# Feed-forward of a hybrid decoder layer: engines in program order, weight splits three products ahead

## The chip, the cores and the metric

The kernel runs on one core of a Trainium2 chip. The metric is the device time of one execution in microseconds (us), the median of several runs. A profiled execution gives the trace from which all other times here are read.

## The reference

One layer of a causal decoder over 2048 tokens of width 1024, in float32:

```
h = x + W_out [ GLA_heads(n) ; DilatedSWA_heads(n) ],  n = RMSNorm(x)
h = h + W_ff2 ( relu( RMSNorm(h) W_ff1 ) ** 2 )        # W_ff1: 1024 x 4096, W_ff2: 4096 x 1024
y = RMSNorm_final(h)
```

Both mixers (gated linear attention and dilated sliding-window attention) lie ahead of everything that is changed. The change concerns the second line and the final norm.

## The kernel before

**Splits.** Every float32 operand of a matrix product is kept as two parts: a high half, rounded by a copy on ScalarE (line 415), and a low half, the difference, made by a subtraction on VectorE (line 416). `mm3` (lines 135 to 137) then makes three matmuls of each block: high by high, low by high, high by low. So a product can start when its high half is there, and goes on when the low half is.

**First feed-forward matrix.** It is multiplied by a scheme with seven products in place of eight, on blocks of two by two. A group is one weight block of 256 columns (`g`, 32 groups: 16 weight blocks for each half of the tokens); its seven products (`j` in the order 1, 2, 5, 6, 3, 4, 7) are numbered through by `at`, 0 to 223. One product is 12 matmuls into one PSUM bank; eight banks go round.

`prep1(at)` makes the split of the weights of product `at` into one of four slots, so it waits until product `at - 4` has been read. Weight differences for later products of the group are made in place in the raw block by VectorE: line 1159 with the second product, lines 1161 and 1162 with the third, 1164 with the fourth. With the seventh product the load of the block two groups on is issued (line 1144, SyncE's queue); there are two raw blocks.

`product1(at)` issues the matmuls and takes the result out of PSUM: by a copy on ScalarE for the first, third and sixth product of a group (line 1191), by additions on VectorE for the others (lines 1193, 1196 and 1197, 1199, and 1202 to 1204 for the seventh). Finished quarters are run through relu and square on ScalarE (lines 1187 and 1188): one quarter with the second and fifth product, two with the seventh.

**Token sums.** The second matrix uses a scheme with 26 products on blocks of the tokens, so the activations are summed over token blocks: 28 sums for each pair of groups, on GpSimd (line 1229), in the tiles `acc1` and in the free halves of `xt` and `gM` (shown as gs), with stores to memory by SyncE (line 1219). They run three steps a product, spread over the pair of groups that follows.

**Reload.** With the last group of the first token half the other operand is replaced by that of the second half: seven loads (line 1110) and 14 split parts (lines 415 and 416, tile hb), between products 106 and 116.

**Second matrix.** 52 phases of eight steps, two blocks of three matmuls a step. Token splits (`prep_s`, lines 1299 to 1303, tile cs, three slots), weight combinations on GpSimd (`add_t`, line 1322), weight splits (`prep_t`, tile ct, six slots), loads, and the additions of results (`taken`, line 1369) are hung on numbered steps by `at_step`; `step(n)` issues what is due, ahead of that step's matmuls. The first of these steps fall into the last 14 products of the first matrix.

**What sets the order.** Each engine works its queue in order. For most of the program a planner decides that order: it simulates the program and picks the next instruction of each engine by its own estimate. Inside `tc.manual_schedule(engines=...)` the named engines keep the order in which the program issues their instructions. In the kernel before, from the first product on, this holds for SyncE alone:

```
    with tc.manual_schedule(engines={SP.engine}):
        ...
        for at in range(7, len(jobs1)):
            ...
            prep1(at + 2)
            product1(at)
            for _ in range(3):
                next(ts, None)
```

`T`, `V`, `A`, `G` and `SP` are TensorE, VectorE, ScalarE, GpSimd and SyncE.

Of the kernel before, what the change touches and what calls it, by code (L numbers as in the profile page):

```python
# [109 lines left out]
def emit(tc, a, stop=99):  # L110
    nc = tc.nc
    V, A, G, T, SP = nc.vector, nc.scalar, nc.gpsimd, nc.tensor, nc.sync
# [9 lines left out]
    def slot(name, dt=F32, n=SLOT):  # L122

        return up.tile([128, SLOT], dt, name=name, tag="u", bufs=26)[:, :n]

    def view(t, shape):
        n = int(np.prod(shape))
        names = "abcd"[:len(shape)]
        return t[:, :n].rearrange(f"p ({' '.join(names)}) -> p {' '.join(names)}", **dict(zip(names, shape)))
# [284 lines left out]
    def split(hi, lo, src):  # L414
        A.activation(hi, src, AF.Copy)  # L415
        V.tensor_tensor(lo, src, hi.bitcast(F32), op=OP.subtract)  # L416
# [4 lines left out]
    X = {}  # L421
# [89 lines left out]
    def reload(j):  # L511
        t = (xp, bp)[order.index(j) % 2][:, :2048]
        SP.dma_start(t, nTD[j - 1].rearrange("p c s -> p (c s)"))

        def rest():
            for cs in (slice(0, 1024), slice(1024, 2048)):
                split(*[v[:, cs] for v in TF[j]], t[:, cs])

        return rest
# [565 lines left out]
    def norm_to_T(src, dst, t):  # L1085

        normed(src, dst, gM)
        half, i = t // HT, t % 4
        b = [view(bb[:, 512 * q:], (4, 128)) for q in range(4)]
        k = t % HT // 4  # L1090
        for q, pv in enumerate(transposed(dst)):
            A.activation(b[2 * k + q], pv, AF.Copy)
        if k == 0:
            return
        (b11, b21, b12, b22), (t2, t4, t3) = b, [view(tb[:, 512 * q:], (4, 128)) for q in range(3)]
        V.tensor_tensor(b12, b12, b11, op=OP.subtract)
        V.tensor_tensor(t2, b22, b12, op=OP.subtract)
        V.tensor_tensor(t4, b21, t2, op=OP.subtract)
        V.tensor_tensor(t3, t2, b11, op=OP.subtract)
        for j, v in ((1, b11), (2, b21), (5, b12), (6, t2), (3, b22), (4, t4), (7, t3)):  # L1100
            SP.dma_start(hTD[half, j - 1][:, :, i * 128:i * 128 + 128], v)
# [37 lines left out]
    def load_w1(g):  # L1139
        if g < 2 * NP:  # L1140
            if len(raw1) < 2:
                raw1.append(view(slot("w1raw"), (CH, 256)))
            g0 = g % NP * 256
            SP.dma_start(raw1[g % 2], w1[:, :, g0:g0 + 256])

    def prep1(at):

        if at >= len(jobs1):
            return
        g, j = jobs1[at]  # L1150
        if not combs1:
            combs1.extend(view(c[:, 1024 * q:], (2, 4, 128)) for c in [slot("w1comb", FR) for _ in range(2)]
                          for q in range(2))
        r = raw1[g % 2]
        (a11, a12), (a21, a22) = [[r[:, 4 * k:4 * k + 4, n * 128:n * 128 + 128] for k in range(2)] for n in range(2)]
        c = combs1[at % 4]
        split(c[:, 0], c[:, 1], {1: a11, 2: a12, 5: a21, 6: a21, 3: a12, 4: a22, 7: a21}[j])
        if j == 2:
            V.tensor_tensor(a21, a21, a22, op=OP.add)  # L1159
        if j == 5:  # L1160
            V.tensor_tensor(a21, a21, a11, op=OP.subtract)  # L1161
            V.tensor_tensor(a12, a12, a21, op=OP.subtract)
        if j == 6:
            V.tensor_tensor(a21, a22, a21, op=OP.subtract)
        if j == 7:
            load_w1(g + 2)
# [3 lines left out]
    def bank():  # L1170
        tags.append(tags.pop(0))
        return ps(tags[-1])

    def product1(at):
        g, j = jobs1[at]
        half, gh = divmod(g, NP)
        if not acc1:
            acc1.extend(slot("acc1") for _ in range(4))
        X = gM[:, :512] if g % 2 else xt[:, :512]
        c11, c12, c21, c22 = [acc1[g % 4][:, 512 * n:512 * n + 512] for n in range(4)]  # L1180
        p = bank()
        B, W = TB[j], combs1[at % 4]
        for c in range(4):
            mm3(p, W[:, 0, c], W[:, 1, c], B[0][:, c], B[1][:, c], c == 0, c == 3)

        def square(v):
            A.activation(v, v, AF.Relu)  # L1187
            A.activation(v, v, AF.Square)

        if j in (1, 5, 4):  # L1190
            A.activation({1: X, 5: c22, 4: c21}[j], p, AF.Copy)
        elif j == 2:
            V.tensor_tensor(c11, p, X, op=OP.add)
            square(c11)
        elif j == 6:
            V.tensor_tensor(X, p, X, op=OP.add)
            V.tensor_tensor(c12, X, c22, op=OP.add)
        elif j == 3:
            V.tensor_tensor(c12, p, c12, op=OP.add)  # L1199
            square(c12)  # L1200
        else:
            V.tensor_tensor(X, p, X, op=OP.add)
            V.tensor_tensor(c21, c21, X, op=OP.add)
            V.tensor_tensor(c22, c22, X, op=OP.add)
            square(c21)
            square(c22)
# [7 lines left out]
    def token_sums(g):  # L1214

        half, c, t = g // NP, g % NP // 2, act_tiles(g)

        def store(r, v):
            SP.dma_start(actD[r, half, :, c], v)

        for i in range(len(SUMS) + BEHIND):
            if i == 2:
                for l, r in SINGLES:
                    store(r, t[l])
            if i >= BEHIND and SUMS[i - BEHIND][4] is not None:
                store(SUMS[i - BEHIND][4], t[SUMS[i - BEHIND][0]])
            if i < len(SUMS):
                l, x, op, y, _ = SUMS[i]
                G.tensor_tensor(t[l], t[x], t[y], op=OP.add if op == "+" else OP.subtract)  # L1229
            yield  # L1230
# [161 lines left out]
    def step(n):  # L1392
        now[0] = n
        for f, args in steps.pop(n, ()):
            f(*args)
# [21 lines left out]
    with tc.manual_schedule(engines={SP.engine}):  # L1417
        rb.append(slot("rb"))
        back = [*back, reload(order[3], 0), reload(order[4], 0), reload(order[5], 0, slot("rt"))]
        load_w1(1)  # L1420
        for at in range(7):
            if at == 2:
                norm_to_T(*late)
            if back:
                list(back.pop(0))
            if at == 1:
                back.append(reload(order[6], 0))
            prep1(at + 2)
            product1(at)


        first, parts_at = 7 * (NP - 1), {}
        for n in range(14):
            parts_at.setdefault(first + 1 + n * 4 // 5, []).append(n // 2)
        halves, begun = {}, set()
        ts = iter(())
        for at in range(7, len(jobs1)):
            if at == first - 2:
                halves.update({n: reload(order[n], 1) for n in range(2)})
            prep1(at + 2)  # L1440
            product1(at)
            for _ in range(3):
                next(ts, None)
            if at % 14 == 13:
                ts = token_sums(at // 7)
            for n in parts_at.get(at, ()):
                next(halves[n])
                if n in begun and n + 2 < 7:
                    halves[n + 2] = reload(order[n + 2], 1)
                begun.add(n)  # L1450
            for n in range(2):
                step(2 * (at - len(jobs1)) + n)

        P, left = {}, None
        for ph in range(2 * NR):
            if PRODUCTS[ph // 2][1]:
                P[ph % 2] = [bank() for _ in range(2)]
            p = P[ph % 2]
            for k in range(8):
                step(8 * ph + k)  # L1460
                if ph < 4:
                    for _ in range(2 - k % 2):
                        next(ts, None)
                if left and k < 2:
                    taken(ph - 1, k, left[k])
                if ph < 2 * NR - 1 or k < 2:
                    for i in range(2):
                        mm2(p[i], ph, k, i)
            left = p
        for i in range(2):  # L1470
            for k in range(2, 8):
                mm2(left[i], 2 * NR - 1, k, i)
            taken(2 * NR - 1, i, left[i])
# [55 lines left out]
```

## Time and profile before

| what | value |
|---|---|
| median of 3 runs | 2422.37 us (2422.12 to 2425.93) |
| profiled execution | 2425.41 us |
| its span, first to last instruction | 2423.6 us |
| first feed-forward matrix, TensorE | 1124.6 to 1827.9 us |
| second feed-forward matrix, TensorE | 1820.3 to 2416.6 us |
| busy share of the span | TensorE 94%, VectorE 70%, GpSimd 49%, ScalarE 48% |
| mean granted TensorE clock | 0.983 |

How the lines are read. A row of busy time by stretches gives the stretch in us and its length, then for each engine (TensorE, its weight loads, VectorE, ScalarE, GpSimd) the busy us and the number of instructions, then the granted clock, the share of the DMA engines and GB/s. A row of waits gives who waited for whom, the us in total, the number of times, and the longest. A row in order of time gives the start and the length in us, engine, line, operation, what it writes and reads, the shapes, how many instructions are merged, and in brackets the idle time of the engine before it and what ended it. A row of a group gives the count, the busy us and the mean in ns, the idle time before them and what ended it; a row by source line gives shortest, median and longest in ns, and the first and last start. PE is TensorE, PEld its weight load, DVE VectorE, ACT ScalarE, POOL GpSimd, SPq SyncE's queue. L416 is line 416.

### The profile page before, as it was taken

To read this page: it belongs to the slowest core of one execution; us is meant where nothing else is said; L and a number is where in the kernel's file an instruction comes from. 1 tells how busy PE (TensorE), PEld (TensorE's weight loads), DVE (VectorE), ACT (ScalarE), POOL (GpSimd) and SP (SyncE) were. 2 spreads that over 40 slices of the span, in tenths; PEclk is the share of its full clock that TensorE was granted. 3 is DMA by queue.
4 is the path that set the end of the run, shared out by engine and by line. 5 is a ranking of instruction groups with operands and counts; after the bars stand their busy time and mean duration, and the time that the engine had idled before them with its cause. 6 is when DMAs were issued, how large, how long until landed. Compare 5 with 4: busy or idle time off the path is not lost.

```text
span 2423.6 us, 35461 instructions
## 1 busy us (share of the span) xinstructions
PE 2288.7 (94%) x12456; PEld 1956.2 (81%) x12456; DVE 1702.2 (70%) x2802; ACT 1165.8 (48%) x2227; POOL 1182.6 (49%) x1098
## 2 busy tenths in 40 slices
PE   6999999999999998999999988899989999999998
PEld 6977998789999996888877776777767778888777
DVE  6888768766676784447666668565667858858786
ACT  5565436435677771235544446444444334333444
POOL 4333324345478784000476576575664635432564
PEclk9999999999999998999999999999999999999999
DMA  6458744767666873677343455444449554444463
GB/s 155 121 162 251 245 147 122 247 186 238 188 215 227 255 238 117 208 258 227 109 131 121 130 158 195 126 125 139 126 132 328 212 189 159 139 156 130 160 225 111
DMA packets 340368, 430.76 MB, mean 178 GB/s; under 512 B 20772, under 2 KB 270133, under 8 KB 333662
## 3 DMA queue, kind: packets, MB, share of 16 engines
q1 hardware_dynamic: 340046, 428.24, 55.4%
q8 instruction: 98, 1.61, 0.3%
q14 instruction: 80, 0.66, 0.1%
q10 hardware_dynamic: 144, 0.26, 0.0%
HBM read 276.60 MB, written 156.54 MB: 179 GB/s over the span
## 4 chain that ended last, share of the span: by engine, by line
PE 48%; POOL 17%; issue 14%; DVE 10%; DMA 8%; ACT 2%; SPq 2%; POOLq 0%; DVEq 0%; ACTq 0%
POOL acc L1229 8%; PE ps_a L136 5%; PE ps_a L137 5%; PE ps_a L135 5%; PE ps_a L753 4%; POOL gs L1229 3%; PE ps_c L136 3%; PE ps_c L137 3%; PE ps_c L135 3%; PE ps_d L734 3%; DMA rt<-w_ff 2%; PE ps_c L712 2%; PE ps_c L714 2%; DVE ct L416 2%; POOL xt L1229 2%
## 5 line engine op out<-in xcount | busy, mean ns | idle before, releaser
L416 DVE TENSOR_TENSOR w1comb<-w1raw,w1comb 128x512 fp32r<-128x512 f32 x224 | 188.9, 846 | 66.2 <-ACT w1comb L415 66.0
L415 ACT ACTIVATE w1comb<-w1raw 128x512 fp32r<-128x512 f32 x224 | 134.9, 623 | 189.3 <-DVE w1raw L1161 167.1
L725 ACT ACTIVATE pe<-pe,O 128x256 f32<-128x256 f32 (+1 forms) x384 | 156.0, 454 | 56.8 <-DVE O L724 52.2
L753 PE MATMUL ps_a<-v,pt 128*128 128x65 f32 x1200 | 178.7, 250 | 0.7 <-DVE pt L743 0.7
L1299 ACT ACTIVATE cs<-rs 128x1024 fp32r<-128x1024 f32 x104 | 108.5, 1049 | 144.9 <-PE ps_c L137 79.4
L753 PEld LDWEIGHTS ps_a<-v,pt 128*128 128x128 f32 x1200 | 174.6, 193 | 2.2 <-DVE pt L743 0.9
L1229 POOL TENSOR_TENSOR acc<-acc 128x256 f32<-128x256 f32 x160 | 168.5, 1066 | 15.5 <-DMA actD<-acc 15.4
L163 POOL TENSOR_TENSOR stats<-stats,mhalf 128x1 f32<-128x1 f32 (+1 forms) x64 | 45.8, 717 | 255.6 <-DVE stats L162 255.5
L416 DVE TENSOR_TENSOR ct<-rt,ct 128x1024 fp32r<-128x1024 f32 x68 | 120.7, 1783 | 59.9 <-ACT ct L415 59.6
L734 PE MATMUL ps_d<-ident,pe 128*128 128x128 f32 x600 | 159.1, 278 | 0.0
L724 DVE CUSTOM_DVE_ANT_0 pe<-ps_c,nb 128x256 f32<-128x256 f32 (+1 forms) x384 | 126.8, 360 | 42.6 <-PE ps_d L734 18.1
L1187 ACT ACTIVATE acc<-acc 128x512 f32<-128x512 f32 x128 | 80.3, 631 | 142.2 <-DVE acc L1199 72.0
L136 PE MATMUL ps_c<-hb,w1comb 128*128 128x512 f32 x336 | 134.3, 400 | 11.7 <-DVE w1comb L416 11.7
L271 ACT ACTIVATE wcomb<-wraw 128x512 fp32r<-128x512 f32 (+2 forms) x126 | 96.5, 772 | 93.9 <-POOL wraw L277 20.5
L136 PE MATMUL ps_c<-ct,cs 128*128 128x512 f32 x360 | 141.2, 392 | 0.4 <-DVE cs L1303 0.4
L137 PE MATMUL ps_c<-ct,cs 128*128 128x512 f32 x360 | 141.3, 392 | 0.0
L135 PE MATMUL ps_c<-ct,cs 128*128 128x512 f32 x360 | 141.0, 392 | 0.0
L135 PE MATMUL ps_c<-hb,w1comb 128*128 128x512 f32 x336 | 133.5, 397 | 7.5 <-ACT w1comb L415 7.5
L415 ACT ACTIVATE ct<-rt 128x1024 fp32r<-128x1024 f32 x68 | 71.5, 1059 | 132.8 <-POOL rt L1322 79.5
L137 PE MATMUL ps_c<-hb,w1comb 128*128 128x512 f32 x336 | 133.2, 396 | 0.0
L273 DVE TENSOR_TENSOR wcomb<-wraw,wcomb 128x512 fp32r<-128x512 f32 (+2 forms) x84 | 100.5, 1200 | 38.0 <-ACT wcomb L271 37.6
L1159 DVE TENSOR_TENSOR w1raw<-w1raw 128x512 f32<-128x512 f32 x32 | 26.2, 819 | 138.3 <-DMA w1raw<-w_ff 137.2
(375 smaller groups left out, 7916.4 us busy)
## 6 DMA issues: line engine op xcount, KB each, us to landing
rs<-actD SPq DMA_DIRECT2D x103, 512.0 KB, 4.3
actD<-acc SPq DMA_DIRECT2D x288, 128.0 KB, 2.1
w1raw<-w_ff SPq DMA_DIRECT2D x32, 1024.0 KB, 6.6
rt<-w_ff SPq DMA_DIRECT2D x24, 1024.0 KB, 8.3
k<-kD SPq DMA_DIRECT2D x16, 1024.0 KB, 8.3
rb<-hTD SPq DMA_DIRECT2D x13, 1024.0 KB, 6.9
wraw<-w_in SPq DMA_DIRECT2D x48, 256.0 KB, 3.7
cmb<-boD SPq DMA_DIRECT2D x16, 528.0 KB, 6.1
```

The lines of the kernel that those rows point to most:

```text
L135: T.matmul(out, sh, mh, start=first, stop=False, skip_group_check=more)
L136: T.matmul(out, sl, mh, start=False, stop=False, skip_group_check=more)
L137: T.matmul(out, sh, ml, start=False, stop=last, skip_group_check=more)
L273: V.tensor_tensor(lo, src, hi.bitcast(F32), op=OP.subtract)
L415: A.activation(hi, src, AF.Copy)
L416: V.tensor_tensor(lo, src, hi.bitcast(F32), op=OP.subtract)
L724: V.tensor_tensor_reduce(p, s, bias, scale=1.0, scalar=BIG, op0=OP.add, op1=OP.min, accum_out=nm)
L725: A.activation(p, p, AF.Exp, bias=nm, scale=-1.0)
L734: T.transpose(pb[:, i * 128:i * 128 + 128], src, ident)
L753: T.matmul(self.b.opsum[:, n % 4], self.pt[:, i * 128:i * 128 + 128], self.b.v[:, blk, cols], start=first, stop=last)
L1229: G.tensor_tensor(t[l], t[x], t[y], op=OP.add if op == "+" else OP.subtract)
L1299: A.activation(v[:, 0, cs], x, AF.Copy, scale=float(sign))
```

## The change

The loop over products splits into two blocks. The first seven products stay as they were ordered (SyncE alone in program order), but from the fourth on `prep1` runs three products ahead there; at the third the splits of both the fifth and the sixth are made, so that none is left out. From the eighth product on, through the second matrix to the end, all five engines keep program order, and `prep1` runs three products ahead.

```
@@ -1425,10 +1425,12 @@
                 list(back.pop(0))
             if at == 1:
                 back.append(reload(order[6], 0))
-            prep1(at + 2)
+            prep1(at + 2 + (at > 2))
+            if at == 2:
+                prep1(5)
             product1(at)
 
-
+    with tc.manual_schedule(engines={X.engine for X in (T, V, A, G, SP)}):
         first, parts_at = 7 * (NP - 1), {}
         for n in range(14):
             parts_at.setdefault(first + 1 + n * 4 // 5, []).append(n // 2)
@@ -1437,7 +1439,7 @@
         for at in range(7, len(jobs1)):
             if at == first - 2:
                 halves.update({n: reload(order[n], 1) for n in range(2)})
-            prep1(at + 2)
+            prep1(at + 3)
             product1(at)
             for _ in range(3):
                 next(ts, None)
```

The four weight slots are not changed, so a split three ahead goes into the slot of the product just before the one being issued.

More of the change, by code (lines that the diff above doesn't have):

```diff
@@ L1427, in emit @@
                 back.append(reload(order[6], 0))
-            prep1(at + 2)
+            prep1(at + 2 + (at > 2))
+            if at == 2:
+                prep1(5)
             product1(at)
+    with tc.manual_schedule(engines={X.engine for X in (T, V, A, G, SP)}):
         first, parts_at = 7 * (NP - 1), {}
@@ L1439, in emit @@
                 halves.update({n: reload(order[n], 1) for n in range(2)})
-            prep1(at + 2)
+            prep1(at + 3)
             product1(at)
```

## The prediction

> **What bounds the kernel now.** I read the page first, then the busy time by stretches, TensorE's waits in the two feed-forward products, then VectorE's, ScalarE's and SyncE's rows in order of time.
>
> ```profile
> span 2423.6 us, 35461 instructions
> 2000.00:2100.00 100.00, 100.00 (x443) 82.81 (x442) 83.32 (x61) 37.63 (x38) 54.14 (x19) 1.00 0.47 155
> 1828.00:2416.00 588.00, 573.31 (x2494) 471.35 (x2493) 448.35 (x394) 230.91 (x278) 275.06 (x130) 0.99 0.53 179
> 1165.00:1203.00 38.00, 38.00 (x169) 31.47 (x168) 26.77 (x33) 20.95 (x36) 27.37 (x28) 1.00 0.38 120
> 1417.00:1514.00 97.00, 85.08 (x338) 65.12 (x337) 76.62 (x86) 51.78 (x85) 63.60 (x56) 0.95 0.58 189
> PE ps_a L136 <- DVE w1comb L416: 24.6, 13, 3.5
> PE ps_c L136 <- DVE w1comb L416: 11.7, 8, 3.9
> PE ps_d L136 <- DVE w1comb L416: 10.3, 8, 2.8
> PE ps_d L136 <- DVE cs L1301: 5.8, 3, 2.4
> PE ps_d L136 <- DVE cs L1303: 4.4, 2, 3.2
> PE ps_a L136 <- DVE cs L1303: 2.2, 1, 2.2
> PE ps_d L135 <- ACT cs L1299: 1.9, 1, 1.9
> ```
>
> A fully fed TensorE issues 443 matmuls in 100 us, 0.2257 us each. So a product of the first feed-forward matrix (12 matmuls) is 2.71 us, a group of seven 18.96, a pair of groups (the period of the token sums) 37.9; the stretch from 1165 shows one such pair. The second matrix has 2494 matmuls in 588 us where 563 would do: it loses 25 us, 14.3 of them in the four waits listed last. The first three waits are the first matrix's: TensorE stands before the low halves that line 416 makes on VectorE.
>
> ```profile
> 1294.42 0.69 DVE L1159 TENSOR_TENSOR w1raw<-w1raw 128x512 f32<-128x512 f32 x1 [8.61 <-DMA w1raw<-w_ff]
> 1330.97 0.40 SPq L1144 DMA_DIRECT2D w1raw<-w_ff  x1
> 1337.79 0.69 DVE L1159 TENSOR_TENSOR w1raw<-w1raw 128x512 f32<-128x512 f32 x1 [8.04 <-DMA w1raw<-w_ff]
> 1338.40 0.68 DVE L416 TENSOR_TENSOR w1comb<-w1raw,w1comb 128x512 fp32r<-128x512 f32 x1
> 1339.90 0.63 ACT L415 ACTIVATE w1comb<-w1raw 128x512 fp32r<-128x512 f32 x1 [8.42 <-DVE w1raw L1161]
> ```
>
> Why they are late: the planner puts line 1159 of the next weight block ahead of the current block's splits. That block's load is issued only at 1330.97, behind stores of token sums in SyncE's queue; VectorE stands 8.04 us in order, and ScalarE 8.42 behind it. Two such rows, one pair apart, lie 43.4 us apart: the steady pair loses 5.5 us against 37.9.
>
> **The change part by part.** Program order sets line 1159 six products later than the planner does, behind the splits of its own block, so this 8 us wait goes. What is late next? In program order each product puts on VectorE: its eviction, the low half four products on, the weight differences. On ScalarE: copy or two squarings, then the high half four products on. The low half waits for the high half, which stands behind the squarings, which wait for the eviction: VectorE and ScalarE take turns. The price of a turn:
>
> ```profile
> 1322.19 0.68 DVE L1193 TENSOR_TENSOR acc<-ps_a,gs 128x512 f32<-128x512 f32 x1
> 1322.90 0.63 ACT L1187 ACTIVATE acc<-acc 128x512 f32<-128x512 f32 x1 [0.84 <-DVE acc L1193]
> 1323.57 0.63 ACT L1188 ACTIVATE acc<-acc 128x512 f32<-128x512 f32 x1
> 1324.10 0.58 ACT L1191 ACTIVATE acc<-ps_c 128x512 f32<-128x512 f32 x1
> 1324.58 1.66 ACT L415 ACTIVATE w1comb<-w1raw 128x512 fp32r<-128x512 f32 x3
> 1325.23 0.77 DVE L416 TENSOR_TENSOR w1comb<-w1raw,w1comb 128x512 fp32r<-128x512 f32 x1 [1.77 <-ACT w1comb L415]
> ```
>
> From the eviction's start to the squaring's end-of-issue 1.91 (1324.10), then the high half 0.63 and 0.03: 2.57 us until the low half starts. Independent VectorE operations of 0.68 start 0.61 apart (1337.79 and 1338.40; I use 0.60), ScalarE's 0.52 (three in 1.66).
>
> ```profile
> 1311.91 1.13 DVE L1159 TENSOR_TENSOR w1raw<-w1raw 128x512 f32<-128x512 f32 x1 [2.10 <-DMA w1raw<-w_ff]
> 1318.75 1.22 DVE L416 TENSOR_TENSOR w1comb<-w1raw,w1comb 128x512 fp32r<-128x512 f32 x1
> 1320.00 1.11 DVE L1164 TENSOR_TENSOR w1raw<-w1raw 128x512 f32<-128x512 f32 x1
> 1327.13 1.22 DVE L1197 TENSOR_TENSOR acc<-gs,acc 128x512 f32<-128x512 f32 x1
> L1203 DVE TENSOR_TENSOR acc<-acc,xt x16: 689/1222/1226, 1147.6 to 1803.9; 128x512 f32<-128x512 f32 x16
> L1203 DVE TENSOR_TENSOR acc<-acc,gs x16: 682/684/693, 1166.2 to 1830.2; 128x512 f32<-128x512 f32 x16
> L1229 POOL TENSOR_TENSOR acc<-acc 128x256 f32<-128x256 f32 x160 | 168.5, 1066 | 15.5 <-DMA actD<-acc 15.4
> ```
>
> The same line 1203 takes 0.68 when it falls where GpSimd has no sums (tile gs, the pair's end) and 1.22 when it falls among them (tile xt). So a group costs twice. Without sums, from the seventh product's eviction: lines 1202 to 1204 and both pairs of squarings, low half at 4.48; difference 5.20; next low half 5.80; L1193 6.40, a turn, low half 8.97; next 9.97 (its high half stands behind a copy); L1196 and L1197 from 10.57; low half 11.88; L1199 12.48, a turn, 15.05; L1159 15.65, whose result the next high half reads: low half 17.01; L1161 17.73, L1162 18.45; next eviction at 19.05. That is TensorE's own 18.96. Among the sums, of the 14 operations of a group that read SBUF twice, 9 are long (over 1 us) in the group whose first and last long ones are the rows at 1311.91 and 1327.13; two of them I take to lie behind ScalarE's part, so 7 x 0.52 = 3.6 is added: 22.7. Bounds: 4 long ones (only those directly behind another) 21.1, 11 of them 24.8. The 28 sums of a pair last 28 x 1.07 = 30 us, in which 30 / 22.7 x 3.6 = 4.8 is added: a pair is 2 x 19.05 + 4.8 = 42.9 (bounds 41.1 and 45.0) against 43.4. The wait for the load goes, and the turns take nearly all of its place.
>
> Three products ahead instead of two covers one late pass: a low half is needed 8.1 us after its slot came free, and the longest pass (seventh product: 3 evictions, 4 squarings, the split) is about 7. It cannot cover a rate, so TensorE's lead is used up once. It also moves the load of line 1144 one product forward in SyncE's queue, past three steps of the sums (some 3 us). Today's load lands just ahead of 1337.79, and in program order its first reader is the split in the turn of the fourth product of the pair, which TensorE reaches 4 x 3.1 us after 1331: some 5 us are left, so the move gains nothing; were the load that much later, the old wait would be back in a smaller size. The sums on GpSimd already run in program order, SyncE too. The extra split in the first seven products (0.62 + 0.68 us) falls on engines that no product waits for yet: nothing; without that cover 0.7.
>
> Terms for the first matrix. Ten ordinary pairs: 10 x (42.9 - 43.4) = -5 (-23 to +16). Two early pairs that run at 38 today: 2 x 4.9 less the lead of 8.1: +2. The reload of the second half's operand:
>
> ```profile
> L416 DVE TENSOR_TENSOR hb<-rb,hb 128x1024 fp32r<-128x1024 f32 x14 | 19.9, 1448 | 6.1 <-ACT hb L415 6.1
> L415 ACT ACTIVATE hb<-rb 128x1024 fp32r<-128x1024 f32 x14 | 14.2, 1049 | 12.4 <-DMA rb<-hTD 12.4
> ```
>
> 14 parts stand in the turns: each adds its 1.4 on VectorE and, after a squaring, 0.4 more until its high half is there, 1.7 on average: 24 us. Today they cost 97.0 - 2 x 43.4 = 10 (the stretch of 338 matmuls, two pairs). So +14 (0 if they fit into VectorE's pauses, +17 at long durations). The last pair takes in six splits of the second matrix, today already partly ahead: +2 (0 to 5). Sum +13.
>
> The second matrix. Program order keeps the split of the weights (line 416, tile ct) behind the token split (cs) of the same stretch; the planner does not:
>
> ```profile
> 2347.48 4.74 POOL L1322 TENSOR_TENSOR rt<-rt 128x1024 f32<-128x1024 f32 x2 [3.80 <-DMA rt<-w_ff]
> 2350.99 2.31 DVE L416 TENSOR_TENSOR ct<-rt,ct 128x1024 fp32r<-128x1024 f32 x1 [5.09 <-ACT ct L415]
> 2356.76 4.52 DVE L1303 SCALAR_TENSOR_TENSOR cs<-rs,cs 128x1024 fp32r<-128x1024 f32 x2
> 2358.03 0.80 PE L136 MATMUL ps_d<-ct,cs 128*128 128x512 f32 x1 [3.21 <-DVE cs L1303]
> 2358.62 0.63 PE L137 MATMUL ps_d<-ct,cs 128*128 128x512 f32 x1
> 2359.05 0.63 PE L135 MATMUL ps_c<-ct,cs 128*128 128x512 f32 x1
> 1880.49 4.76 POOL L1322 TENSOR_TENSOR rt<-acc,rt 128x1024 f32<-128x1024 f32 x2 [13.92 <-DMA acc<-w_ff]
> ```
>
> Here VectorE stands for a late combination on GpSimd and only then makes the token split that TensorE awaits; in the program's order the token split comes first. TensorE then runs at 0.43 us per matmul for a while: the waits are 14.3 of the 25 us, these slow matmuls the rest, and I count all 25 as removed. Against it, one combination is late by itself (1880.49, its load waits for the last token sums' tile), and in program order a token split stands behind it: +4 (0 to 10). Together -21 (-25 to -15).
>
> By the Trainium skill (TensorE: Matmul & The Clock Gate, Part 1) the array falls back to half rate only after about 3.4 us of idleness. The rows show half rate after waits of 1.90 and 3.21 us; by the page the removed waits would return 14 us, not 25, and the kernel would end 11 us later than I forecast.
>
> Sum: +13 - 21 = -8 against the profiled run's own 2425.4 us: 2417. The median of the runs shown, 2422.4, lies 3 us lower: 2414.
>
> **The rivals.** *The turns never bind* (0.15). If VectorE needs 19.05 us among the sums too, a pair is 38.1: 10 x -5.3 = -53, early pairs 0, reload +4, second matrix -21: -70, 2352. For it: the early pair at 38.00 with 28 sums in it, in the planner's order. Against it: that order batches two high halves after a squaring, the new one cannot.
>
> *The turns are longer than the load's wait* (0.22). 11 long operations: 45.0 a pair: +16, early pairs +6, reload +17, end +2, second matrix -21: +20, 2442. It decides from a pair of about 43.6 us up: there the sum is zero, and each 0.1 more costs 1.2 us.
>
> *The second matrix gives nothing back* (0.15). If the late combinations now hold ScalarE's queue, token splits wait behind weight splits in other places: 13 + 0 = +13, 2435. For it: line 1322 waits for loads again and again; against it: an earlier token split also frees its load in SyncE's queue earlier. That the order stays what it was is excluded by the two rows of line 1159.
>
> **How the numbers follow.** My forecast has 0.48, by itself 2396 to 2432 by the bounds of its ten pairs. Of it 0.32 lies more than 4.8 us (0.2%, about what this kernel's measurement can tell) below the median, 0.10 within, 0.06 above. The fast rival adds 0.15; of the long turns 0.02 and of the second matrix's rival 0.04 lie within 0.2%, the rest above: faster 0.47, same 0.16, slower 0.37. The range 2372 to 2444 cuts off the far ends of the fast and the slow rival.
>
> **What would show it.** VectorE's waits at line 1159 for the load gone; ScalarE's high halves (line 415) right behind line 1188, VectorE before line 416 waiting for them about 1.9 us three times a group; TensorE waiting once or twice a pair for w1comb still, most among the sums and around the reload; hardly any wait of TensorE for cs, but one near the second weight combination. A pair under 40 or over 44.5 us, or TensorE's waits for cs as large as now, would prove me wrong.

## The result, and the profile after

The changed kernel takes 2449.72 us (median of 4 runs, 2446.52 to 2452.52). The kernel before, beside it on the same chip, takes 2422.24 us (4 runs, 2420.77 to 2425.93). The ratio is 1.0111, 95% interval 1.0093 to 1.0128: the change costs 27 us. The forecast was 2414, the range 2372 to 2444. The profiled execution's span grew from 2423.6 to 2447.5 us.

First the page of the changed kernel, its span and the group of the first matrix's low halves. The first number behind the bar is the busy time in us, the second the mean of one in ns; behind the next bar stands the idle time ahead of them.

```profile
span 2447.5 us, 35592 instructions
...
L416 DVE TENSOR_TENSOR w1comb<-w1raw,w1comb 128x512 fp32r<-128x512 f32 x224 | 205.3, 918 | 195.8 <-ACT w1comb L415 195.6
```

Two rows of waits of the kernel before, over its first feed-forward matrix (us in total, times, longest):

```profile
DVE w1raw L1159 <- DMA w1raw<-w_ff: 134.8, 28, 9.5
...
DVE w1comb L416 <- ACT w1comb L415: 66.0, 46, 2.2
```

And the rows of the changed kernel that answer to them:

```profile
DVE w1comb L416 <- ACT w1comb L415: 195.6, 129, 2.5
ACT acc L1187 <- DVE acc L1203: 130.0, 31, 5.5
ACT acc L1187 <- DVE acc L1193: 89.8, 31, 4.9
...
PE ps_a L135 <- ACT w1comb L415: 19.5, 9, 4.1
...
PE ps_c L135 <- ACT w1comb L415: 15.1, 6, 4.0
...
PE ps_c L136 <- DVE w1comb L416: 7.6, 7, 2.6
```

VectorE's 134.8 us before the load are gone: the changed kernel has no wait of line 1159 for it. In their place VectorE stands 195.6 us for ScalarE's high halves, and ScalarE 219.8 us (130.0 and 89.8) for VectorE's evictions (lines 1203 and 1193). The two engines take turns, and TensorE now stands mostly for the high half, before mostly for the low one.

One turn of the changed kernel, in order of time:

```profile
1351.86 0.68 DVE L1193 TENSOR_TENSOR acc<-ps_o,xt 128x512 f32<-128x512 f32 x1
1352.57 0.63 ACT L1187 ACTIVATE acc<-acc 128x512 f32<-128x512 f32 x1 [2.77 <-DVE acc L1193]
...
1353.24 0.63 ACT L1188 ACTIVATE acc<-acc 128x512 f32<-128x512 f32 x1
...
1353.77 0.62 ACT L415 ACTIVATE w1comb<-w1raw 128x512 fp32r<-128x512 f32 x1
...
1354.42 2.14 DVE L416 TENSOR_TENSOR w1comb<-w1raw,w1comb 128x512 fp32r<-128x512 f32 x2 [1.89 <-ACT w1comb L415]
```

From eviction to low half 2.56 us, 1.89 of them idle on VectorE. Busy time by stretches of the changed kernel: the first matrix, one ordinary pair in it, the second matrix, and its two parts.

```profile
1127.40:1848.40 721.00, 660.98 (x2700) 529.70 (x2697) 497.43 (x599) 344.78 (x597) 396.26 (x421) 0.94 0.44 139
1298.90:1343.00 44.10, 41.53 (x170) 33.54 (x169) 30.02 (x37) 20.40 (x36) 26.25 (x28) 0.92 0.41 128
1848.40:2440.50 592.10, 575.91 (x2496) 473.28 (x2495) 466.44 (x398) 233.29 (x279) 270.56 (x131) 0.98 0.53 175
1860.00:2300.00 440.00, 440.00 (x1943) 364.45 (x1942) 349.13 (x288) 162.87 (x172) 200.12 (x89) 1.00 0.54 177
2300.00:2441.00 141.00, 124.59 (x508) 99.98 (x506) 109.11 (x104) 62.55 (x97) 65.59 (x38) 0.93 0.48 156
```

The first matrix grew from 703.3 to 721.0 us (+17.7), the second, from the end of the first, from 588.7 to 592.1 (+3.4); 2.8 us are there before the first product that the change touches. The second matrix is remarkable: from 1860 to 2300 TensorE has no gap at all, and from 2300 on it loses everything that it had won. TensorE's largest waits there (1860 to the end):

```profile
PE ps_d L136 <- DVE cs L1303: 4.4, 2, 4.0
PE ps_c L136 <- DVE cs L1301: 4.0, 1, 4.0
PE ps_a L135 <- ACT cs L1299: 3.0, 1, 3.0
...
```

All of its waits there, 16.0 us, are for token splits, and all but 0.4 us fall right behind finished rows of the output. One such place, in order of time:

```profile
2341.69 0.67 DVE L1369 TENSOR_TENSOR sum<-sum,ps_c 128x512 f32<-128x512 f32 x1
2342.45 0.63 ACT L1346 ACTIVATE gs<-sum 128x512 f32<-128x512 f32 x1 [5.82 <-DVE sum L1369]
...
2343.21 0.16 DVE L1352 TENSOR_TENSOR stats<-oss 128x1 f32<-128x1 f32 x1 [0.85 <-ACT gs L1346]
...
2343.64 0.55 POOL L163 TENSOR_TENSOR stats<-stats,mhalf 128x1 f32<-128x1 f32 x1 [5.22 <-DVE stats L162]
...
2344.22 0.75 DVE L1354 SCALAR_TENSOR_TENSOR sum<-sum,stats,gs 128x512 f32<-128x512 f32 x1 [0.66 <-POOL stats L163]
2344.89 0.68 DVE L1369 TENSOR_TENSOR sum<-sum,ps_o 128x512 f32<-128x512 f32 x1
...
2347.36 5.13 POOL L1322 TENSOR_TENSOR acc<-rt,acc 128x1024 f32<-128x1024 f32 x2
...
2347.43 2.85 DVE L1354 SCALAR_TENSOR_TENSOR sum<-sum,stats,gs 128x512 f32<-128x512 f32 x1 [0.66 <-POOL stats L163]
...
2350.20 3.38 DVE L1303 SCALAR_TENSOR_TENSOR cs<-rs,cs 128x1024 fp32r<-128x1024 f32 x1
...
2353.63 0.79 PE L136 MATMUL ps_d<-ct,cs 128*128 128x512 f32 x1 [3.98 <-DVE cs L1303]
```

A row of output is a round trip: VectorE adds, ScalarE squares, VectorE adds two scalars, GpSimd takes the root, VectorE scales. From the addition at 2341.69 to the next addition at 2344.89 that is 3.2 us of VectorE's queue in which it works 1.7. In program order two rows stand one behind the other, 8.5 us in all, and the token split that TensorE needs at about 2349 begins at 2350.20.

The trips are not the whole of it. Of the 8.5 us VectorE is idle for 3.0. Another 2.1 are the second scaling, 2.85 us where the first took 0.75, and the token split behind it takes 3.38 us, where the one at 2354.64 takes 1.21. Both long operations lie beside GpSimd's weight combination of 2347.36. So idle time and lengthened operations both go into TensorE's wait of 3.98 us.

### The profile page after: what moved, and what is told of

It reads as the page before. It is cut to its first block, busy times and chain, and to the rows that moved or that the text cites. A ratio compares the mean times of both kernels' runs of the same rounds, so it can differ in the third digit from the quotient of the medians.

```text
span 2447.5 us, 35592 instructions
## 1 busy us (share of the span) xinstructions
PE 2309.2 (94%) x12456; PEld 1972.9 (81%) x12456; DVE 1737.4 (71%) x2802; ACT 1169.1 (48%) x2227; POOL 1150.4 (47%) x1098
## 4 chain that ended last, share of the span: by engine, by line
PE 50%; issue 15%; POOL 13%; DMA 10%; DVE 9%; ACT 3%; SPq 0%; POOLq 0%; DVEq 0%; ACTq 0%
POOL acc L1229 8%; PE ps_a L137 5%; PE ps_a L136 5%; PE ps_a L135 5%; PE ps_a L753 4%; PE ps_c L135 4%; PE ps_c L136 4%; PE ps_c L137 4%; PE ps_d L734 3%; POOL gs L1229 2%; PE ps_c L712 2%; PE ps_c L714 2%; PE ps_d L136 2%; PE ps_d L137 2%; PE ps_d L135 2%
## 5 line engine op out<-in xcount | busy, mean ns | idle before, releaser
L416 DVE TENSOR_TENSOR w1comb<-w1raw,w1comb 128x512 fp32r<-128x512 f32 x224 | 205.3, 918 | 195.8 <-ACT w1comb L415 195.6
L1229 POOL TENSOR_TENSOR acc<-acc 128x256 f32<-128x256 f32 x160 | 161.7, 1018 | 7.3 <-DMA actD<-acc 4.8
L135 PE MATMUL ps_c<-hb,w1comb 128*128 128x512 f32 x336 | 137.2, 408 | 19.0 <-ACT w1comb L415 15.1
L1229 POOL TENSOR_TENSOR xt<-acc,acc 128x256 f32<-128x256 f32 x32 | 23.7, 740 | 275.9 <-ACT acc L1188 266.7
L416 DVE TENSOR_TENSOR ct<-rt,ct 128x1024 fp32r<-128x1024 f32 x68 | 129.9, 1911 | 26.0 <-ACT ct L415 25.9
L136 PE MATMUL ps_c<-hb,w1comb 128*128 128x512 f32 x336 | 138.1, 411 | 7.6 <-DVE w1comb L416 7.6
L137 PE MATMUL ps_c<-hb,w1comb 128*128 128x512 f32 x336 | 137.1, 408 | 1.4 <-DVE hb L416 1.4
L273 DVE TENSOR_TENSOR wcomb<-wraw,wcomb 128x512 fp32r<-128x512 f32 (+2 forms) x84 | 100.6, 1203 | 36.2 <-ACT wcomb L271 35.7
L1303 DVE SCALAR_TENSOR_TENSOR cs<-rs,cs 128x1024 fp32r<-128x1024 f32 (+1 forms) x56 | 101.1, 1808 | 28.4 <-ACT cs L1299 28.4
```

The lines of the kernel that those rows point to most:

```text
L135: T.matmul(out, sh, mh, start=first, stop=False, skip_group_check=more)
L136: T.matmul(out, sl, mh, start=False, stop=False, skip_group_check=more)
L137: T.matmul(out, sh, ml, start=False, stop=last, skip_group_check=more)
L1303: V.scalar_tensor_tensor(v[:, 1, cs], x, -1.0, v[:, 0, cs].bitcast(F32), op0=OP.mult, op1=OP.subtract)
```

## The experiments

Theory 1 after the result: two separate causes, the turns of VectorE and ScalarE in the first matrix and the output rows' round trips in the second. Differences below are against the kernel before in the same session (medians 2425.1, 2424.4 and 2426.2 us in the three sessions).

### Program order in one matrix alone

Program order and three products ahead for the first matrix; the second as before:

```
+    with tc.manual_schedule(engines={SP.engine}):
         P, left = {}, None
```

> The first feed-forward matrix is as in the changed kernel; in the second one SyncE alone keeps program order, as in the kernel before. Theory 1 (two separate causes: turns of VectorE and ScalarE cost the first matrix 18 us, and in the second matrix old and new losses are nearly equal, 25 and 26 us): the first matrix stays near 721 us, the second goes back from 592 to about 589 us, in all about 2446 us. Theory 2 (one cause: the outputs' round trips in program order; the first matrix's 18 us are read wrongly or belong to this execution): the planner puts token splits between them, the 26 us go, about 2424 us.

Measured 2451.07 us (4 runs), ratio 1.0109 (1.0095 to 1.0124).

```profile
1127.20:1846.20 719.00, 656.68 (x2699) 525.86 (x2697) 496.90 (x598) 342.97 (x595) 397.34 (x422) 0.94 0.44 139
1846.20:2441.30 595.10, 575.97 (x2497) 471.69 (x2496) 453.35 (x398) 235.03 (x282) 280.22 (x130) 0.99 0.53 174
```

Theory 2 falls: the first matrix is as slow (719.0 us, 15.7 more than before), and the planner's order brings its own stalls back in the second (595.1 us, some 6 more than the 589 expected; why was not followed up). So the changed order of the first matrix alone makes the kernel as slow as the whole change does.

The other way round, program order from the second matrix on only (against the kernel before, so splits stay two products ahead):

```
+    with tc.manual_schedule(engines={SP.engine}):
         first, parts_at = 7 * (NP - 1), {}
 ...
+    with tc.manual_schedule(engines={X.engine for X in (T, V, A, G, SP)}):
         P, left = {}, None
```

> The first matrix is as in the kernel before (splits two products ahead, SyncE alone in order); all engines keep program order only from the second matrix's first phase on. Theory 1: the second matrix exchanges the stalls of the planner's order (25 us) for those at the output rows (26 us), so it takes about 592 us and the whole about 2426 us. Theory 2 (the second matrix's stalls at the output rows come from a backlog that it takes over from the first matrix): they don't appear, and about 2397 us is left.

Measured 2438.71 us (6 runs, 2428.99 to 2441.56), ratio 1.0050 (1.0034 to 1.0066). The stalls at the output rows are there without any change of the first matrix, so theory 2 falls. The second matrix took 593.4 us, as theory 1 says, but the median is 13 us over its figure, while the profiled execution, 2428.99, was near it. So this kernel was profiled once more:

> The kernel in which all engines keep program order from the second matrix on, unchanged, once more: its profiled execution had taken 2429.0 us, the five others 2436 to 2442 us. If those hold a stall that the first profile lacks, this profile is near 2438 us and shows it; if it is near 2429 us, the gap stays open.

Measured 2443.2 us (one run). The stretch ahead of the first feed-forward product in both profiles, then both matrices of the second:

```profile
0.00:1121.60 1121.60, 1070.76 (x7265) 968.52 (x7265) 768.98 (x1802) 589.98 (x1350) 483.33 (x545) 0.99 0.65 201
```

```profile
0.00:1132.40 1132.40, 1076.46 (x7265) 974.63 (x7265) 774.89 (x1802) 589.73 (x1350) 482.62 (x545) 0.98 0.64 200
1132.40:1835.50 703.10, 643.25 (x2701) 518.19 (x2699) 478.63 (x603) 343.91 (x598) 421.33 (x421) 0.96 0.45 140
1835.50:2434.10 598.60, 578.43 (x2496) 472.53 (x2494) 461.31 (x395) 230.97 (x278) 269.32 (x131) 0.98 0.54 176
```

The second profile's span is 14.1 us longer. Of this 10.8 us lie ahead of everything that was changed, with the same number of instructions on every engine, and 5.2 in the second matrix. Why the mixers ran longer in this execution stays open. What both profiles agree on is that the second matrix in program order is 5 to 10 us longer than before, not 21 shorter. The costs of the two halves alone, 26 and 14 us, are not terms of a sum: the whole change costs 27.

### Two products ahead in program order, three in the planner's

The first keeps program order from the eighth product on and goes back to two products ahead (against the kernel before):

```
+    with tc.manual_schedule(engines={X.engine for X in (T, V, A, G, SP)}):
         first, parts_at = 7 * (NP - 1), {}
```

> All engines keep program order as in the changed kernel, but the weight splits are made two products ahead throughout, as before. Theory 1 (what binds among the sums is the rate of the turns, so the distance only moves the place where TensorE stands): the ordinary pair stays at 44 us or gets 0 to 2 us longer, since a split has 5.4 instead of 8.1 us from the squarings to its product; 2450 to 2475 us. Theory 2 (the third product's distance carries the gain that there is): each seventh product's pass of about 7 us is late by 1.6 us or more in every group, 32 groups, about 2500 us or more.

Measured 2448.80 us (5 runs), ratio 1.0102 (1.0084 to 1.0120): the same as the changed kernel. By TensorE's starts the pairs take 43.7 to 44.4 us, outside the first, the last and the two of the reload, in nearly equal groups of about 21.7 and 22.2 where the changed kernel mostly has 19.0 and 25. In program order a rate binds, and the distance only decides where in the pair TensorE stands.

The second keeps three ahead and lets the planner order again:

```
-    with tc.manual_schedule(engines={X.engine for X in (T, V, A, G, SP)}):
+    with tc.manual_schedule(engines={SP.engine}):
```

> Splits three products ahead, but SyncE alone keeps program order, as in the kernel before. Theory 1 (distance gains nothing, since the planner's VectorE still stands for the load of the weight block, which is now issued one product earlier in SyncE's queue): the pair stays near 43.4 us, 2418 to 2427 us. Theory 2 (distance is the useful half of the change): the pair goes down by up to 2.7 us, 2385 to 2400 us.

Measured 2404.84 us (5 runs), ratio 0.9916 (0.9903 to 0.9928): 20 us faster than before. It lies between the theories, 13 us under the first and 5 over the second.

```profile
DVE w1raw L1159 <- DMA w1raw<-w_ff: 108.6, 28, 8.2
```

VectorE still stands for the load, 108.6 us against 134.8, and the first matrix takes 682.6 us (1128.2 to 1810.8) against 703.3, with pairs of 41.1 to 42.0 us ahead of the reload. I read it so: a stall that comes once a pair can be bridged in part by a lead that is rebuilt within the pair; a rate cannot. This is not shown. With three ahead the load of line 1144, which stands in `prep1`, is issued one product earlier too, and VectorE's wait for it became 26 us shorter; no run separates the distance from the earlier load. What is shown is that the change joins two edits of opposite sign: three ahead in the planner's order gains 20 us, program order with two ahead costs 24, and both together cost 27, so that nothing is left of the 20.

### What makes the pair 44 us: turns, or GpSimd's sums

The squares held back by one product, behind its weight split, so that no high half waits for an eviction:

```
+    held = []
+    def squares():
+        for v in held:
+            A.activation(v, v, AF.Relu)
+            A.activation(v, v, AF.Square)
+        held.clear()
 ...
-        def square(v):
-            A.activation(v, v, AF.Relu)
-            A.activation(v, v, AF.Square)
+        square = held.append
 ...
             prep1(at + 3)
+            squares()
             product1(at)
 ...
```

Two more calls of `squares()`, behind each of the first seven products and ahead of the second matrix, are left out of this listing.

> The changed kernel, but relu and square of a finished quarter are issued one product later, behind that product's weight split, so ScalarE makes the high half without waiting for VectorE's addition. Theory 1 (turns: in an ordinary pair VectorE is busy about 30 us and stands about 14 us before line 416 for the high halves): the waits go, VectorE's 30 us fit under TensorE's 37.9 us, the pair falls from 44 to 38 or 39 us, 13 such pairs give 65 to 78 us and the reload some more: 2360 to 2390 us. Theory 2 (VectorE's rate beside GpSimd binds, and the waits are only where it rests): the pair stays above 42.5 us, 2430 to 2450 us.

Measured 2354.85 us (4 runs), ratio 0.9714 (0.9696 to 0.9732): 69.5 us faster than before, and some 97 faster than the changed kernel. In this kernel's trace line 1178 is the relu and 1179 the square. A stretch of one pair, the first matrix and the second:

```profile
1204.70:1242.80 38.10, 38.10 (x170) 31.55 (x169) 29.93 (x37) 20.88 (x36) 27.14 (x28) 1.00 0.47 145
...
1126.30:1753.80 627.50, 617.14 (x2700) 506.72 (x2699) 499.81 (x600) 353.94 (x598) 417.83 (x421) 0.99 0.51 159
1753.80:2346.50 592.70, 575.29 (x2496) 472.26 (x2494) 462.39 (x397) 232.40 (x278) 272.97 (x131) 0.98 0.54 175
```

Every pair but the first and that of the reload is 38.1 us, TensorE's own time, with the same 28 sums beside it and the same 30 us of VectorE (30.02 in the changed kernel, 29.93 here). Its wait before line 416, in that pair and in a pair of the changed kernel:

```profile
DVE w1comb L416 <- ACT w1comb L415: 7.3, 5, 1.8
```

```profile
DVE w1comb L416 <- ACT w1comb L415: 14.3, 10, 2.5
```

In the changed kernel 30.0 of work and 14.3 of waiting fill VectorE's 44.1 us. With the squares held back half the waiting is left, and TensorE, busy 38.10 of 38.10 us, loses nothing by it.

The counter-test leaves the turns and takes the sums away.

```
-                G.tensor_tensor(t[l], t[x], t[y], op=OP.add if op == "+" else OP.subtract)
 ...
+        for v in (xt, gM):
+            G.memset(v[:, 512:], 0.0)
```

> The changed kernel without the 28 token sums of each pair of groups (line 1229 left out, its stores kept, the free halves of xt and gM set to zero once): the output is no longer the layer's. Theory 1 (the turns cost nothing at VectorE's and ScalarE's short durations, and only their lengthening beside GpSimd's sums makes a pair 44 us): VectorE's operations keep to 0.68 us, a pair takes 38.1 us, the first matrix about 640 us, in all about 2370 us. Theory 2 (the turns alone are longer than TensorE's work): the pair stays at 41 us or more, over 2405 us.

Measured 2364.48 us (4 runs), ratio 0.9755 (0.9739 to 0.9772). One pair, and VectorE's wait in it:

```profile
1203.20:1241.30 38.10, 38.10 (x170) 31.54 (x169) 23.26 (x37) 20.31 (x36) 0.00 (x0) 1.00 0.47 146
```

```profile
DVE w1comb L416 <- ACT w1comb L415: 15.2, 11, 2.5
```

Theory 1 holds. The turns are all there, 15.2 us of waiting in a pair (0.7 of it ahead of the stretch), and TensorE loses nothing. VectorE's 23.3 us of work and this waiting fill the 38.1 us, so the turns just fit, as the prediction's 19.05 us a group without sums has it. With the sums VectorE's same 37 operations take 30 instead of 23.3 us, and with about the same waiting a pair is 44. Either cause alone is free; together they are 6 us a pair.

The sums might also have held up ScalarE itself: in the changed kernel 14 of its waits before line 1187, 59.2 us, are put down to GpSimd's line 1229. But each of the 14 ends 0.76 us after the start of VectorE's eviction of line 1199, as other turns do (0.71 in the one shown), so it was the eviction that ended them.

Then the distance with the turns gone, two products ahead:

> The kernel with the squares held back by one product, program order for all engines, but splits two products ahead. Theory 1 (once no engine waits in turns, VectorE's and ScalarE's work fits under TensorE's and 5.4 us suffice for a split; the third product of distance is needed only where the operand is reloaded): ordinary pairs stay at 38.1 us, 2355 to 2362 us. Theory 2 (the distance of three is what makes the held squares work): the seventh product's split is late in each group, a pair takes 40 us or more, over 2380 us.

```
             prep1(at + 2)
+            squares()
             product1(at)
```

Measured 2352.05 us (5 runs), ratio 0.9705 (0.9685 to 0.9724), ordinary pairs 38.1 us. Theory 1 holds: the distance is not needed. And held squares with three ahead in the planner's order:

> The squares held back by one product and splits three products ahead, but SyncE alone keeps program order. Theory 1 (the planner goes by its own estimate, whatever the order of issue; it still puts line 1159 ahead of the splits and VectorE stands for the load): about 2400 to 2410 us, as with three ahead alone. Theory 2 (the order in which the squares are issued is what matters, program order is not needed): below 2375 us.

```
             prep1(at + 3)
+            squares()
             product1(at)
 ...
-    with tc.manual_schedule(engines={X.engine for X in (T, V, A, G, SP)}):
+    with tc.manual_schedule(engines={SP.engine}):
```

Measured 2406.34 us (6 runs), ratio 0.9920 (0.9903 to 0.9936), as with three ahead alone: the planner makes its own order and still waits for the load.

```profile
DVE w1raw L1159 <- DMA w1raw<-w_ff: 110.5, 28, 9.5
```

So program order is needed for the gain, with the order of issue put right.

### The output rows

In the changed kernel, the root two steps behind the squares, scaling and stores five steps behind:

```
+        n = now[0]
+        if n < 16 * NR - 10:
+            r = []
+            at_step(n + 2, lambda: r.append(root(col)))
+            at_step(n + 5, lambda: scaled(half, m, i, C, r[0]))
+        else:
+            scaled(half, m, i, C, root(col))
 ...
```

`root` and `scaled` hold the lines that stood here before.

> The changed kernel, but of a finished output row the root (lines 1351 and 1352) is issued two steps behind the squares and the scaling and stores (lines 1354 to 1359) five steps behind, except for the last rows. Theory 1 (TensorE's stalls from 2300 us on come from the round trips VectorE, ScalarE, VectorE, GpSimd, VectorE that stand ahead of the next token split): most of the 26 us of waits and slow matmuls there go, about 2425 to 2430 us. Theory 2 (the additions, the weight splits and GpSimd's late combinations fill the engines there anyway): the stalls stay, 2445 to 2452 us.

Measured 2440.20 us (6 runs), ratio 1.0066 (1.0051 to 1.0082): 12 us better than the changed kernel, between the two theories.

```profile
1847.20:2429.20 582.00, 571.73 (x2497) 468.63 (x2495) 465.06 (x398) 232.16 (x280) 281.83 (x131) 1.00 0.54 178
```

The second matrix falls from 592.1 to 582.0 us; at 0.2257 us a matmul its 2496 would take 563.3, so 28.8 us of loss became 18.7. So issuing the root and the scaling later gives back 10 us of it. In the rest are 10.1 us of waits, still for token splits in the same region, each 1.6 us or shorter.

Both edits together:

> Both edits of the two kernels before. Theory 1 (two independent causes): their gains add up, 2335 to 2365 us, below the kernel before by 60 to 85 us. Theory 2 (a faster first matrix brings the second one's loads and combinations into trouble, or one cause covers the other): the gains don't add up, over 2375 us.

Measured 2345.88 us (5 runs, 2340.63 to 2349.86), ratio 0.9673 (0.9656 to 0.9690): 78 us faster than before and the fastest of all.

```profile
1125.50:1753.90 628.40, 618.48 (x2699) 507.52 (x2698) 500.18 (x600) 353.80 (x598) 416.95 (x421) 0.99 0.51 159
1753.90:2335.40 581.50, 571.27 (x2497) 468.54 (x2495) 461.60 (x397) 231.31 (x278) 277.74 (x131) 1.00 0.55 179
```

The gains add up: 628.4 and 581.5 are the first matrix of the one and the second matrix of the other, within 1 us. In the second matrix one candidate for what is left can be read in order of time:

```profile
2248.01 5.81 POOL L1328 TENSOR_TENSOR acc<-rt,acc 128x1024 f32<-128x1024 f32 x2
...
2248.69 5.69 DVE L1371 SCALAR_TENSOR_TENSOR sum<-sum,stats,gs 128x512 f32<-128x512 f32 x2
```

Two scalings of rows that now lie side by side beside GpSimd's weight combinations take 5.7 us. The next token split starts late behind them, and TensorE waits 1.5 and 1.6 us for it at 2258.54 and 2260.64. Whether moving them off the combinations would return the rest was not tried.

## Why the prediction was wrong, point by point

The terms of the sum against the profiled executions (pairs from TensorE's first matmul of each; the ten ordinary pairs took 43.7 us each before, not the 43.4 that the prediction read from two rows of line 1159):

| term | forecast | measured |
|---|---|---|
| ten ordinary pairs | -5 (42.9 each) | +1.4 (43.9 each) |
| two early pairs | +2 | +9.5 |
| reload, two pairs | +14 | +11.5 |
| last pair | +2 | -4.6 |
| first matrix | +13 | +17.7 |
| second matrix | -21 | +3.4 |
| ahead of the changed part | 0 | +2.8 |

**The step that failed is the second matrix,** -21 in the sum and +3.4 measured. "I count all 25 as removed" was right for what it named up to 2300 us: there the stalls of the planner's order are gone, 440.00 busy us in a stretch of 440.00, and the +4 for the late combination did not come either. What I put at nothing is what program order adds. I followed token splits and weight splits through the new order and did not follow the output rows through it: their round trip of 3.2 us, twice in series, stands ahead of a token split. TensorE's waits for cs were to be hardly any, and as large as before would prove me wrong: they are 16.0 us against 14.7. I had asked of program order in the first matrix who takes turns with whom; the same question in the second would have found line 1346 waiting for 1369 and 1354 for 163. The term is 24 of the 33 us between the profiled run and its forecast of 2417. Of the 28.8 us that the second matrix now loses, the moved output rows gave back 10; for the rest the trace shows round trips and operations lengthened beside GpSimd's combinations, and no run separates the two.

**The turns were right, the length of a pair a little short.** A turn was forecast at 2.57 us and took 2.56; the waits at line 1159 are gone; the high half follows line 1188; VectorE waits 1.89 us; TensorE stands for w1comb in some two places a pair. A group among the sums was forecast at 22.7, and one traced from 1344.36 took 22.75; the one after it took 21.2 where the sums' remainder was counted to 20.2. So a pair is 43.9 and not 42.9; by the place of the excess, the sums reach further into the second group than I counted, which no run isolated. The second rival put its point at 43.6, and the pair fell on its side of it; but it also had 45.0, which it did not reach.

**The lead of 8.1 us did not show.** The early pairs were to lose 9.8 and get 8.1 back. They lost 9.5. Two ahead and three ahead in program order take the same time (2448.8 and 2449.7 us), so the lead is worth nothing measurable there. In the planner's order three ahead, with the earlier load, is worth 20 us: "it cannot cover a rate" fits, but I had not asked what it is worth without the other half of the change.

**The reload** at +14 was near (+11.5); the last pair became 4.6 us shorter where I had expected 2 more; no run isolated that. That the first matrix came near as a whole, +17.7 against +13, is in part luck: the early pairs lay 7.5 us over their term and the last pair 6.6 under.

**The rivals.** The third, the second matrix giving nothing back, forecast 2435 and its sum was the nearest in kind: +13 and 0 against +17.7 and +3.4. Its mechanism, late combinations holding ScalarE's queue, is not what happened: from 1860 to 2300 there is no stall, and the large waits after it stand behind output rows. The first, turns that never bind, is refuted for this kernel, but its condition is what the held squares bring about.

**Half rate.** Between 1860 and 2276 the kernel before shows

```profile
1860.00:2276.00 416.00, 407.64 (x1778) 335.30 (x1777) 317.74 (x256) 150.71 (x152) 179.23 (x67) 0.99 0.50 167
```

1778 matmuls at 0.2257 us are 401.3, so 14.7 us were lost, 8.4 of them idle. The changed kernel has no gap from 1860 to 2300, so the slow matmuls behind the waits went with the waits, and the prediction's larger count holds there. Its wait of 1.90 us was weak evidence, since only one matmul lies between it and the one of 3.21. But the wait of 2.00 us at 1954.03 stands alone, and from the second on the matmuls behind it are 0.43 us apart; behind the 2.18 us at 1924.39 they are 0.22 to 0.24 apart. By the Trainium skill (TensorE: Matmul & The Clock Gate, Part 1) the half rate comes after an idle window of about 3.4 us. This trace has it behind 2.00 us as well.

## What to carry to other kernels

Before giving all engines program order, follow each engine's queue through the program as it is written and list every place where one engine's instruction stands behind another engine's answer; such a round trip can become idle time on both, at the end of the program as well as in the main loop. The waiting that the order forces is free as long as it and the engine's work together stay under the time of the engine that bounds. Work that sum out ahead, as the turns were worked out here, with the durations that hold beside the other engines' work; in a trace work and waiting always fill the time. Then cut the turn by issuing the answer's consumer later, behind the work that TensorE needs next; here holding the squares back by one product was worth some 97 us.

## What the hardware showed that was not expected

Operations of VectorE that read two operands from SBUF took 0.68 us alone and up to 1.22 us beside GpSimd's 256-wide sums, as the prediction had read. Beside GpSimd's 1024-wide combinations the loss is far larger: line 1354 takes 0.75 us at 2344.22 and 2.85 at 2347.43, and line 1303 takes 1.21 us at 2354.64 in the changed kernel and 3.38 at 2350.20.

```profile
2354.64 1.21 DVE L1303 SCALAR_TENSOR_TENSOR cs<-rs,cs 128x1024 fp32r<-128x1024 f32 x1
```

And one kernel in two executions can differ by 10.8 us ahead of its changed part (1121.6 and 1132.4 us for the same 7265 matmuls), four times the 2.8 us that the two profiles compared here show there.
